# Seven block products in place of eight in the first feed-forward matrix, with two of four weight sums made by adding transfers

## The chip, the core and the metric

The kernel runs on one core of a Trainium2 chip. Its engines work side by side and are tied by semaphores: TensorE (PE) multiplies and writes to PSUM, VectorE (DVE) and ScalarE (ACT) work on elements, GpSimd (POOL) does the same more slowly and issues some transfers, SyncE (SP) only issues transfers. The metric is device microseconds (us) of one call, the median of several runs.

## What is computed

```python
def swiglu(x, w_in, w_out):
    gate, up = jnp.split(x @ w_in, 2, axis=-1)          # 1024 -> 2 x 2816
    return (jax.nn.silu(gate) * up) @ w_out             # 2816 -> 1024

def encoder_layer(x, ...):                              # DEPTH = 2
    x = layer_norm(ALPHA * x + 0.5 * swiglu(x, w_ffn_in[0], w_ffn_out[0]), ...)
    ...                                                 # pooling, short convolution, differential attention
    x = layer_norm(ALPHA * x + mix @ w_out, ...)
    x = layer_norm(ALPHA * x + 0.5 * swiglu(x, w_ffn_in[1], w_ffn_out[1]), ...)
```

There are 512 prompt tokens and 32 tokens of a second request, 544 in all, and all of it is float32. Two layers with two feed-forward blocks each make four feed-forward blocks; `w_ffn_in` of one block is 1024 x 5632.

## The kernel before

Activations stand with features on the partitions: 8 tiles `x[k]` of 128 x 544, worked on in two token halves `HS[0]` and `HS[1]` of 272 columns. For precision every operand is split into a high and a low part (`whi`, `wlo`, `xh`, `xl`), and a product is three matmuls: `whi*xh`, `wlo*xh`, `whi*xl` (`mm_h`, `mm_l`). Every matmul of these phases has 128 x 128 weights and 272 columns.

A feed-forward block walks over 22 slices of 128 hidden features (`i` in `ffn`). For each slice it multiplies the gate tile and the up tile of the first matrix: two tiles, two halves, 8 `k`, 3 matmuls, 96 in all. ACT takes silu of the gate (`sg`), DVE multiplies with the up part (L449), and the result is split into `hh` and `hl`. After 8, 7 and 7 slices (`FSPLIT`) the second matrix is multiplied for these slices and added to the residual `y` (one tile `ya` for all `k`). The last such phase is `out_phase`, which interleaves the layer norm `LN`, and `start` begins the next matrix while the normed `x` is still being made.

`Weights` streams the weights: SP loads a tile into one of two `raw` buffers, `group` makes a high part of 512 columns on ACT (L159) and a low part on DVE (L160), in rings of `W_BUFS` = 8 buffers. A ring buffer is written again when the matmuls of the group 8 places earlier have ended. The order of instructions on an engine is set at build time by a scheduler, and each engine executes its list in that order; an instruction that waits holds up everything behind it on its engine.

Of the kernel before, what the change touches and what calls it, by code (L numbers as in the profile page):

```python
# [16 lines left out]
P = 128  # L17
# [11 lines left out]
NF = D_FF // P  # L29
FSPLIT = (8, 7, 7)  # L30
NB = 2
W_BUFS = 8
# [16 lines left out]
UW = 640  # L49

# [17 lines left out]
def encoder_kernel(  # L68
# [28 lines left out]
    tp = ctx.enter_context(tc.tile_pool(name="tp", bufs=4))  # L97
# [46 lines left out]

    class Weights:


        def __init__(self, specs):
            self.specs, self.used, self.loaded, self.ready = specs, 0, 0, []

        def fetch(self):
            self.loaded += 1
            return wp.tile([P, NK * P], F32, tag="raw", name="raw", bufs=RAW_BUFS)

        def group(self, raw, g, n):
            e = min(G, n - g)
            hi = wp.tile([P, G], F32R, tag="whi", name="whi", bufs=W_BUFS)
            lo = wp.tile([P, G], F32R, tag="wlo", name="wlo", bufs=W_BUFS)
            S.activation(out=hi[:, :e], in_=raw[:, g:g + e], func=AF.Copy)  # L159
            V.tensor_tensor(out=lo[:, :e], in0=raw[:, g:g + e], in1=hi[:, :e].bitcast(F32), op=ALU.subtract)  # L160
            return hi, lo

        def load(self):
            src, n = self.specs[self.loaded]
            raw = self.fetch()
            nc.sync.dma_start(out=raw[:, :n], in_=src)
            self.ready.append([self.group(raw, g, n) for g in range(0, n, G)])

        def first(self, x):

            specs = self.specs[:2]
            raws = [self.fetch() for _ in specs]
            self.ready = [[], []]
            for i in range(NK // 4):
                ks, cs = slice(4 * i, 4 * i + 4), slice(i * G, (i + 1) * G)
                nc.sync.dma_start(out=ya[:, ks, HS[0]], in_=xT[:, ks, HS[0]])
                for (src, n), raw in zip(specs, raws):
                    nc.sync.dma_start(out=raw[:, cs], in_=src[:, cs])
                for k in range(NK)[ks]:
                    split(y[k], x[k], HS[0])  # L180
                for raw, out in zip(raws, self.ready):
                    out.append(self.group(raw, i * G, NK * P))
            nc.sync.dma_start(out=ya[:, :, HS[1]], in_=xT[:, :, HS[1]])

        def ahead(self, n):

            while self.loaded < min(self.used + n, len(self.specs)):
                self.load()

        def get(self, n=2):  # L190
# [3 lines left out]

    def mm_h(acc, w, x, k, h, first):

        cs = slice((k % 4) * P, (k % 4) * P + P)
        for i, v in enumerate(w[k // 4]):
            PE.matmul(acc[:, :HALF], v[:, cs], x[k][0][:, HS[h]], start=first and i == 0, stop=False)  # L199

    def mm_l(acc, w, x, k, h, last):

        cs = slice((k % 4) * P, (k % 4) * P + P)
        PE.matmul(acc[:, :HALF], w[k // 4][0][:, cs], x[k][1][:, HS[h]], start=False, stop=last)  # L204
# [30 lines left out]

    class LN:
# [9 lines left out]
        def ln_tile(self, name):  # L246
            return tp.tile([P, T], F32, tag="ln", name=name, bufs=3)

        def half_tile(self, tag, name, bufs):
            return tp.tile([P, HALF], F32, tag=tag, name=name, bufs=bufs)  # L250
# [29 lines left out]
        def add_last(self, m, acc, h):  # L280
            c, q = y[m][:, HS[h]], self.half_tile("z", "sq", 4)
# [23 lines left out]
        def spread(self, h, psum):  # L305

            d = self.half_tile("dg", "diag", 2)[:CH].rearrange("p (c t) -> p c t", c=NCH)
# [10 lines left out]
        def scale(self, h, k):  # L318
            l, j, sl = self.l, self.j, HS[h]
            c = y[k][:, sl]  # L320
            z = self.half_tile("z", "z", 4)
# [25 lines left out]
    def out_phase(l, j, x, ks, alpha):  # L347
# [4 lines left out]
        first = NK - nb  # L352
        for m in range(first):
# [37 lines left out]
        if ln.final:  # L391
# [7 lines left out]
            mean = ln.half_tile("dg", "mean", 2)  # L399
# [13 lines left out]
    def start(x, step, hooks, done):  # L413

        ws = [W.get(0), W.get(0)]
        accs = [(bank(), bank()), (bank(), bank())]
        todo = [(h, k) for h in range(2) for k in range(NK)][done:]
        for h in range(2):
            for k in range(NK):
# [8 lines left out]
                if h == 1 and k in (3, 6):  # L428
                    W.ahead(k // 3)
# [4 lines left out]

    def ffn(l, f, x, pre):
        for s, n in enumerate(FSPLIT):
            hs = []
            for i in range(n):
                if pre:
                    ga, ua = pre  # L440
                    pre = None
# [542 lines left out]
```

## Time and profile before

| what | value |
|---|---|
| median of 3 runs | 2107.07 us (2106.86 to 2107.29) |
| the profiled execution | 2106.86 us, of which the span from first to last instruction is 2104.7 us |
| PE busy | 2079.3 us, 99% of the span |
| DVE busy | 1013.1 us, 48% |
| ACT busy | 771.6 us, 37% |
| POOL busy | 228.8 us, 11% |
| moved by transfers | 189.13 MB, 90 GB/s on average |

Busy time of an engine adds up its instructions, which overlap a little on each engine because they are pipelined. The prediction is made against the span; 2.2 us of the profiled execution lie outside it.

### The profile page before, as it was taken

The numbers are of one execution on the slowest core, as the hardware profiler recorded it, in microseconds if no ns is written. First come the engines' busy times: TensorE is split into PE (matmuls) and PEld (weight loads), VectorE is DVE, ScalarE is ACT, GpSimd is POOL, SyncE is SP. The second block draws the span as 40 slices with busy tenths as digits, with TensorE's granted clock in tenths as the row PEclk, the third lists the DMA queues.
The fourth block names the chain that finished last, engine by engine and source line by source line (L and its number), as shares of the span: only waits on it lengthen the run. The fifth ranks groups of instructions, "written<-read, shape, count | busy, mean of one in ns | idle before, by whom it ended". The sixth has DMA issues, their size and how long they took to land.

```text
span 2104.7 us, 38545 instructions
## 1 busy us (share of the span) xinstructions
PE 2079.3 (99%) x16286; PEld 2042.2 (97%) x16286; DVE 1013.1 (48%) x1970; ACT 771.6 (37%) x1591; POOL 228.8 (11%) x216
## 2 busy tenths in 40 slices
PE   9999999999999999999999999999999999999997
PEld 9999999999999999999999999999999999999997
DVE  4333333776556333333653333347766553333337
ACT  5323223565435323223443232235653353222233
POOL 0000000511133000000420000006011320000003
PEclk9999999999999999999999999999999999999999
DMA  7322222132232222222232222222321222222221
GB/s 240 99 91 83 90 91 84 59 115 92 62 119 81 91 86 86 84 98 82 70 101 83 89 88 89 89 85 67 109 93 54 78 91 82 90 89 82 91 83 61
DMA packets 61749, 189.13 MB, mean 90 GB/s; under 512 B 8932, under 2 KB 13156, under 8 KB 61576
## 3 DMA queue, kind: packets, MB, share of 16 engines
q1 hardware_dynamic: 52592, 173.18, 25.9%
q10 hardware_dynamic: 8984, 13.49, 2.0%
q8 instruction: 128, 2.10, 0.4%
q14 instruction: 45, 0.37, 0.1%
HBM read 179.88 MB, written 8.34 MB: 89 GB/s over the span
## 4 chain that ended last, share of the span: by engine, by line
PE 95%; DVE 2%; POOL 1%; ACT 1%; issue 1%; DMA 0%; SPq 0%; POOLq 0%; ACTq 0%
PE b L199 59%; PE b L204 30%; PE b L629 1%; PE b L628 1%; PE o L644 1%; POOL xl L333 1%; PE b L609 0%; ACT ya L327 0%; DVE z L322 0%; PE b L716 0%; POOL rstd L302 0%; PE b L682 0%; DVE diag L308 0%; DVE acc L286 0%; PE b L311 0%
## 5 line engine op out<-in xcount | busy, mean ns | idle before, releaser
L199 PE MATMUL b<-xh,whi 128*128 128x272 f32 x3456 | 1000.0, 291 | 6.2 <-ACT xh L332 3.7
L199 PE MATMUL b<-xh,wlo 128*128 128x272 f32 x3456 | 993.5, 289 | 0.3 <-DVE wlo L160 0.3
L204 PE MATMUL b<-xl,whi 128*128 128x272 f32 x3456 | 978.2, 288 | 0.2
L160 DVE TENSOR_TENSOR wlo<-raw,whi 128x512 fp32r<-128x512 f32 (+1 forms) x656 | 469.7, 719 | 694.8 <-ACT whi L159 692.7
L159 ACT ACTIVATE whi<-raw 128x512 fp32r<-128x512 f32 (+1 forms) x656 | 403.3, 619 | 858.7 <-PE b L204 569.8
L199 PEld LDWEIGHTS b<-xh,whi 128*128 128x128 f32 x3456 | 651.7, 189 | 9.5 <-ACT xh L332 5.9
L199 PEld LDWEIGHTS b<-xh,wlo 128*128 128x128 f32 x3456 | 653.1, 189 | 1.5 <-DVE wlo L160 0.8
L204 PEld LDWEIGHTS b<-xl,whi 128*128 128x128 f32 x3456 | 644.6, 188 | 2.1 <-POOL xl L333 1.5
L199 PE MATMUL b<-hh,wlo 128*128 128x272 f32 x1408 | 406.2, 289 | 0.0
L199 PE MATMUL b<-hh,whi 128*128 128x272 f32 x1408 | 405.2, 288 | 0.0
L204 PE MATMUL b<-hl,whi 128*128 128x272 f32 x1408 | 404.6, 287 | 0.0
L199 PEld LDWEIGHTS b<-hh,wlo 128*128 128x128 f32 x1408 | 264.9, 188 | 0.2
L204 PEld LDWEIGHTS b<-hl,whi 128*128 128x128 f32 x1408 | 264.9, 188 | 0.2
L199 PEld LDWEIGHTS b<-hh,whi 128*128 128x128 f32 x1408 | 264.9, 188 | 0.0
L278 POOL TENSOR_TENSOR ya<-ya,shift 128x544 f32<-128x544 f32 x14 | 24.8, 1792 | 1412.9 <-DVE wlo L160 1386.4
L448 ACT ACTIVATE sg<-b 128x272 f32<-128x272 f32 x176 | 69.6, 397 | 213.1 <-PE b L204 213.0
L449 DVE SCALAR_TENSOR_TENSOR sg<-b,sg 128x272 f32<-128x272 f32 x176 | 77.6, 441 | 130.9 <-PE b L204 119.2
L343 DVE SCALAR_TENSOR_TENSOR ya<-ya,b 128x272 f32<-128x272 f32 x88 | 38.5, 438 | 88.7 <-PE b L204 87.8
L333 POOL TENSOR_TENSOR xl<-ya,xh 128x272 fp32r<-128x272 f32 x80 | 70.3, 901 | 30.8 <-ACT xh L332 25.1
L345 DVE TENSOR_TENSOR ya<-ya,b 128x272 f32<-128x272 f32 x108 | 46.7, 433 | 54.0 <-PE b L204 53.8
L232 ACT ACTIVATE hh<-sg 128x544 fp32r<-128x544 f32 (+1 forms) x100 | 59.1, 591 | 32.6 <-DVE sg L449 32.5
L233 DVE TENSOR_TENSOR hl<-sg,hh 128x544 fp32r<-128x544 f32 (+1 forms) x100 | 65.2, 652 | 7.2 <-ACT hh L232 7.1
(183 smaller groups left out, 1455.9 us busy)
## 6 DMA issues: line engine op xcount, KB each, us to landing
raw<-in_w SPq DMA_DIRECT2D x206, 512.0 KB, 3.5
raw<-in_w SPq DMA_DIRECT2D x64, 448.0 KB, 3.3
raw<-in_wi SPq DMA_DIRECT2D x40, 512.0 KB, 3.5
raw<-in_wo SPq DMA_DIRECT2D x16, 512.0 KB, 3.5
U<-scr ACTq DMA_DIRECT2D x8, 320.0 KB, 4.8
out_nkT<-k ACTq DMA_DIRECT2D x8, 272.0 KB, 2.1
out_nvT<-vT ACTq DMA_DIRECT2D x8, 272.0 KB, 2.1
out_yT<-ya SPq DMA_DIRECT2D x16, 136.0 KB, 1.8
```

What stands on the lines that cost most here:

```text
L159: S.activation(out=hi[:, :e], in_=raw[:, g:g + e], func=AF.Copy)
L160: V.tensor_tensor(out=lo[:, :e], in0=raw[:, g:g + e], in1=hi[:, :e].bitcast(F32), op=ALU.subtract)
L199: PE.matmul(acc[:, :HALF], v[:, cs], x[k][0][:, HS[h]], start=first and i == 0, stop=False)
L204: PE.matmul(acc[:, :HALF], w[k // 4][0][:, cs], x[k][1][:, HS[h]], start=False, stop=last)
L232: S.activation(out=hh[:, sl], in_=t[:, sl], func=AF.Copy)
L233: (eng or V).tensor_tensor(out=hl[:, sl], in0=t[:, sl], in1=hh[:, sl].bitcast(F32), op=ALU.subtract)
L278: POOL.tensor_tensor(out=c, in0=c, in1=self.s, op=ALU.subtract)
L333: POOL.tensor_tensor(out=xl[:, sl], in0=c, in1=xh[:, sl].bitcast(F32), op=ALU.subtract)
L343: V.scalar_tensor_tensor(out=c, in0=c, scalar=ALPHA, in1=a, op0=ALU.mult, op1=ALU.add)
L345: V.tensor_tensor(out=c, in0=c, in1=a, op=ALU.add)
L448: S.activation(out=sg[:, sl], in_=g[:, :HALF], func=AF.Silu)
L449: V.scalar_tensor_tensor(out=sg[:, sl], in0=u[:, :HALF], scalar=0.5, in1=sg[:, sl], op0=ALU.mult, op1=ALU.mult)
```

## The change

The matrix of one slice is cut into blocks: two token halves of `x`, two halves of the contraction (`k` 0 to 3, `e`; `k` 4 to 7, `o`), and up and gate. Slices 0 and 1 of a block (`NPLAIN` = 2) keep the eight block products. The other 20 slices use seven, each of 4 `k` and 3 matmuls, 12 matmuls. For that, sums are formed of the activations, once per feed-forward block (`Blocks`: `s56`, `s73`), and of the weight blocks, once per slice (`Weights.sums`): two by a transfer that POOL issues and that adds to what is already in its target (`accum_op`), two by DVE (`add`). A slice now has seven weight groups instead of four, and the ring has 9 buffers. The seven products go into three PSUM banks, one of which is read and then accumulated further (`seven`, `hidden`). One slice of the next split is computed ahead of each phase of the second matrix (`plan`). Tiles of the sums share memory with the tiles of attention and are allocated and released around it (`big["pool"]`).

```diff
-W_BUFS = 8
+NPLAIN = 2
+W_BUFS = 9
+XB = 18
...
+        def add(self, a, b):
+            r = big["pool"].tile([P, G], F32, tag="sum", name="sum", bufs=2)
+            V.tensor_tensor(out=r, in0=a, in1=b, op=ALU.add)
+            return r
+
+        def sums(self, src):
+            r13 = big["pool"].tile([P, 2 * G], F32, tag="r13", name="r13", bufs=2)
+            nc.sync.dma_start(out=r13, in_=src[:, :2 * G])
+            r11 = big["pool"].tile([P, G], F32, tag="b11", name="b11", bufs=2)
+            nc.sync.dma_start(out=r11, in_=src[:, :G])
             raw = self.fetch()
+            nc.sync.dma_start(out=raw, in_=src[:, 2 * G:])
+            POOL.dma_start(out=r13, in_=src[:, G:3 * G], accum_op=ALU.add)
+            b22, b21, r1, r3 = raw[:, :G], raw[:, G:], r13[:, :G], r13[:, G:]
+            g11, g21 = self.group(r11), self.group(b21)
+            r2 = self.add(r1, b22)
+            g2, g1 = self.group(r2), self.group(r1)
+            g3 = self.group(r3)
+            g22 = self.group(b22)
+            return g11, g21, g2, g1, g3, g22, self.group(self.add(r2, b21))
...
+    class Blocks:
+        def add(self, e, o):
+            h0, h1 = HS
+            t1, t2 = tmp("s56"), tmp("s73")
+            V.tensor_tensor(out=t1[:, h0], in0=e[:, h1], in1=o[:, h1], op=ALU.subtract)
+            V.tensor_tensor(out=t1[:, h1], in0=t1[:, h0], in1=e[:, h0], op=ALU.subtract)
+            V.tensor_tensor(out=t2[:, h0], in0=e[:, h0], in1=e[:, h1], op=ALU.subtract)
+            V.tensor_tensor(out=t2[:, h1], in0=o[:, h0], in1=t1[:, h1], op=ALU.add)
+            s = [new_b(n) for n in ("s56", "s73")]
+            split(t1, s[0])
+            split(t2, s[1])
+            self.sums.append(s)
+        def products(self):
+            e, o = self.plain[:NK // 2], self.plain[NK // 2:]
+            s56, s73 = ([s[i] for s in self.sums] for i in range(2))
+            for xs, h in ((e, 0), (o, 0), (s56, 1), (s56, 0), (s73, 0), (s73, 1), (o, 1)):
+                yield [tuple(v[:, HS[h]] for v in x) for x in xs]
+
+    def seven(ws, blocks, after):
+        banks = {}
+        for i, (w, xs, name) in enumerate(zip(ws, blocks.products(), "abacaca")):
+            opens = name not in banks
+            acc = banks.setdefault(name, bank() if opens else None)
+            for j, (xh, xl) in enumerate(xs):
+                cs = slice(j * P, (j + 1) * P)
+                for m, (v, x) in enumerate(((w[0], xh), (w[1], xh), (w[0], xl))):
+                    PE.matmul(acc[:, :HALF], v[:, cs], x, start=opens and j == 0 and m == 0,
+                              stop=j == len(xs) - 1 and m == 2, skip_group_check=True)
+            after[i](acc[:, :HALF])
...
+    def hidden(ws, blocks):
+        copy = lambda out: lambda acc: S.activation(out=out, in_=acc, func=AF.Copy)
+        def times(u, sl):
+            V.scalar_tensor_tensor(out=sg[:, sl], in0=u, scalar=0.5, in1=sg[:, sl], op0=ALU.mult, op1=ALU.mult)
+        def c12(acc):
+            V.tensor_tensor(out=sg[:, h0], in0=acc, in1=sg[:, h0], op=ALU.subtract)
+            S.activation(out=sg, in_=sg, func=AF.Silu)
+            times(up, h0)
+        seven(ws, blocks, [
+            copy(up),
+            lambda acc: V.tensor_tensor(out=up, in0=acc, in1=up, op=ALU.add),
+            copy(sg[:, h0]),
+            copy(sg[:, h1]),
+            lambda acc: V.tensor_tensor(out=sg[:, h1], in0=sg[:, h1], in1=acc, op=ALU.subtract),
+            c12,
+            lambda acc: times(acc, h1),
+        ])
+        return sg
...
     def ffn(l, f, x, pre):
+        xb = Blocks(x)
+        hs = []
+        for what, i in plan():
...
+                    sg = hidden(W.get(), xb)
...
-        with tc.tile_pool(name=f"at{l}", bufs=1) as ap:
-            x, pre = mixer(l, x, pre, ap)
+        big["pool"].release()
+        with tc.tile_pool(name=f"at{l}", bufs=1, reuse_waits="tile") as ap:
+            mix = mixer(l, x, pre, ap)
+        big["pool"] = tc.alloc_tile_pool(name="xb", bufs=1, reuse_waits="tile")
+        x, pre = out_phase(l, 1, mix, (4, 5, 6, 0, 1, 2, 3, 7), True)
```

The order of ACT's instructions in the stretch of seven-product slices decides when a PSUM bank is read. Before, one slice (hidden features of `sg_850`) stands on ACT as follows; `whi` are high parts of coming weights.

```order
L448 ACTIVATE sg_850<-b_740 128x272
L159 ACTIVATE whi_861<-raw_859 128x512
L448 ACTIVATE sg_850<-b_741 128x272
L159 ACTIVATE whi_865<-raw_859 128x512
L159 ACTIVATE whi_921<-raw_919 128x512
L159 ACTIVATE whi_925<-raw_919 128x512
L232 ACTIVATE hh_851<-sg_850 128x544
```

Now one slice (`sg_731`) stands there like this; `b_733` is the bank that four of its products share, `b_774` the one of two, and L558 are the copies out of them after the first, third and fourth product.

```order
L174 ACTIVATE whi_709<-sum_707 128x512
L558 ACTIVATE up_732<-b_733 128x272
L174 ACTIVATE whi_713<-r13_692 128x512
L174 ACTIVATE whi_717<-r13_692 128x512
L558 ACTIVATE sg_731<-b_733 128x272
L174 ACTIVATE whi_721<-raw_696 128x512
L558 ACTIVATE sg_731<-b_774 128x272
L174 ACTIVATE whi_727<-sum_725 128x512
L174 ACTIVATE whi_840<-b11_835 128x512
L565 ACTIVATE sg_731<-sg_731 128x544
L174 ACTIVATE whi_844<-raw_837 128x512
L292 ACTIVATE hh_829<-sg_731 128x544
```

A high part now stands ahead of the first copy, and silu and the split of the result share the queue with the parts of the next two slices. DVE had this order for one slice before (the low parts `wlo`, the two multiplications L449, the split L233):

```order
L160 TENSOR_TENSOR wlo_991<-raw_988,whi_990 128x512
L160 TENSOR_TENSOR wlo_995<-raw_988,whi_994 128x512
L449 SCALAR_TENSOR_TENSOR sg_979<-b_929,sg_979 128x272
L160 TENSOR_TENSOR wlo_1051<-raw_1048,whi_1050 128x512
L449 SCALAR_TENSOR_TENSOR sg_979<-b_930,sg_979 128x272
L160 TENSOR_TENSOR wlo_1055<-raw_1048,whi_1054 128x512
L233 TENSOR_TENSOR hl_981<-sg_979,hh_980 128x544
```

and has this one now, from the first weight sum of one slice to that of the next:

```order
L206 TENSOR_TENSOR sum_848<-r13_833,raw_837 128x512
L570 TENSOR_TENSOR up_732<-b_747,up_732 128x272
L175 TENSOR_TENSOR wlo_714<-r13_692,whi_713 128x512
L175 TENSOR_TENSOR wlo_718<-r13_692,whi_717 128x512
L175 TENSOR_TENSOR wlo_722<-raw_696,whi_721 128x512
L573 TENSOR_TENSOR sg_731<-sg_731,b_733 128x272
L175 TENSOR_TENSOR wlo_728<-sum_725,whi_727 128x512
L206 TENSOR_TENSOR sum_866<-sum_848,raw_837 128x512
L564 TENSOR_TENSOR sg_731<-b_774,sg_731 128x272
L175 TENSOR_TENSOR wlo_841<-b11_835,whi_840 128x512
L561 SCALAR_TENSOR_TENSOR sg_731<-up_732,sg_731 128x272
L561 SCALAR_TENSOR_TENSOR sg_731<-b_733,sg_731 128x272
```

and behind these:

```order
L175 TENSOR_TENSOR wlo_845<-raw_837,whi_844 128x512
L293 TENSOR_TENSOR hl_830<-sg_731,hh_829 128x544
L175 TENSOR_TENSOR wlo_851<-sum_848,whi_850 128x512
L206 TENSOR_TENSOR sum_989<-r13_974,raw_978 128x512
```

Fifteen instructions stand where seven stood. The last reader of the buffer `r13_692` is `wlo_718`; the next contents of that buffer are `r13_974`, and `sum_989`, their first reader, stands 12 places behind.

On SP three loads per slice stand where two stood, and POOL adds one transfer per slice that waits for the load of the same buffer (semaphores in brackets):

```order
L213 DMA b11_976<-in_w1 128x512 [waits DMAHW7_49,DMAHW5_49,DVE_49]
L211 DMA r13_974<-in_w1 128x1024 [waits DMASW2_49,DVE_49]
L215 DMA raw_978<-in_w1 128x1024 [waits DMAHW1_49,DVE_49]
...
L216 DMA r13_974<-in_w1 128x1024 [waits DMAHW6_49,DMASW2_49,DVE_49]
```

The first three are SP's, the last is POOL's; before, POOL issued no transfers.

## Rows read from the trace of the kernel before

**Rows 1.** The page's head, its busy times of all engines, the granted clock of PE in 40 slices (tenths of full speed), the main transfer queue (packets, MB, share of 16 engines) and the chain that ended last by engine.

```profile
span 2104.7 us, 38545 instructions
PE 2079.3 (99%) x16286; PEld 2042.2 (97%) x16286; DVE 1013.1 (48%) x1970; ACT 771.6 (37%) x1591; POOL 228.8 (11%) x216
PEclk9999999999999999999999999999999999999999
q1 hardware_dynamic: 52592, 173.18, 25.9%
PE 95%; DVE 2%; POOL 1%; ACT 1%; issue 1%; DMA 0%; SPq 0%; POOLq 0%; ACTq 0%
```

**Rows 2.** What PE waited for: us in total, times, longest wait.

```profile
PE b L311 <- DVE diag L308: 8.2, 6, 2.9
PE b L199 <- ACT xh L332: 3.7, 7, 1.0
```

**Rows 3.** Timeline (start, us, engine, line) of PE in a slice of the first matrix: three matmuls in a row, the first of them the last of a token half, and beside them ACT's silu that waits for that half.

```profile
60.22 0.29 PE L204 MATMUL b<-xl,whi 128*128 128x272 f32 x1
60.35 0.29 PE L199 MATMUL b<-xh,whi 128*128 128x272 f32 x1
60.47 0.29 PE L199 MATMUL b<-xh,wlo 128*128 128x272 f32 x1
60.55 0.40 ACT L448 ACTIVATE sg<-b 128x272 f32<-128x272 f32 x1 [1.77 <-PE b L204]
```

**Rows 4.** Timeline of ACT over one slice; idle time ahead of a row and what ended it stand in brackets.

```profile
62.09 0.63 ACT L159 ACTIVATE whi<-raw 128x512 fp32r<-128x512 f32 x1 [1.14 <-PE b L204]
63.53 0.40 ACT L448 ACTIVATE sg<-b 128x272 f32<-128x272 f32 x1 [0.81 <-PE b L204]
69.59 0.63 ACT L159 ACTIVATE whi<-raw 128x512 fp32r<-128x512 f32 x1 [0.87 <-PE b L204]
70.13 0.64 ACT L232 ACTIVATE hh<-sg 128x544 fp32r<-128x544 f32 x1
72.55 0.40 ACT L448 ACTIVATE sg<-b 128x272 f32<-128x272 f32 x1 [1.77 <-PE b L204]
84.55 0.40 ACT L448 ACTIVATE sg<-b 128x272 f32<-128x272 f32 x1 [1.77 <-PE b L204]
```

**Rows 5.** Timeline of DVE: a low part behind its high part, a low part with the split right behind it, then pairs of equal instructions back to back, first with POOL idle, then with POOL at work.

```profile
62.75 0.70 DVE L160 TENSOR_TENSOR wlo<-raw,whi 128x512 fp32r<-128x512 f32 x1 [3.17 <-ACT whi L159]
70.26 0.69 DVE L160 TENSOR_TENSOR wlo<-raw,whi 128x512 fp32r<-128x512 f32 x1 [0.28 <-ACT whi L159]
70.87 0.72 DVE L233 TENSOR_TENSOR hl<-sg,hh 128x544 fp32r<-128x544 f32 x1
...
662.88 1.29 DVE L160 TENSOR_TENSOR wlo<-raw,whi 128x512 fp32r<-128x512 f32 x2
...
651.81 0.78 DVE L316 TENSOR_TENSOR ya<-ya,b 128x272 f32<-128x272 f32 x2
656.82 1.86 DVE L160 TENSOR_TENSOR wlo<-raw,whi 128x512 fp32r<-128x512 f32 x2
```

**Rows 6.** Groups of instructions by line and shape: count, busy us, mean ns of one.

```profile
L160 DVE TENSOR_TENSOR wlo<-raw,whi 128x512 fp32r<-128x512 f32 x592 | 427.5, 726 | 677.1 <-ACT whi L159 675.0
L449 DVE SCALAR_TENSOR_TENSOR sg<-b,sg 128x272 f32<-128x272 f32 x176 | 77.6, 441 | 130.9 <-PE b L204 119.2 <-ACT sg L448 3.9
```

**Rows 7.** Transfers by line: count, KB each, median us from issue to landing.

```profile
raw<-in_w SPq DMA_DIRECT2D x206, 512.0 KB, 3.5
U<-scr ACTq DMA_DIRECT2D x8, 320.0 KB, 4.8
ya<-in_xT SPq DMA_DIRECT2D x1, 1088.0 KB, 8.6
```

**Rows 8.** Four slices of the first matrix as one stretch: us, busy us of PE, PEld, DVE, ACT and POOL (instructions), granted clock, share of the 16 DMA engines, GB/s.

```profile
168.00:216.00 48.00, 48.00 (x387) 48.00 (x386) 17.19 (x28) 15.03 (x28) 0.00 (x0) 1.00 0.28 87
```

**Rows 9.** Timeline at the end of a layer norm, ahead of the second feed-forward block of layer 0: POOL, ACT (the last normed tiles L327, silu of slice 0 and of slice 1) and DVE (the last centred tiles).

```profile
656.12 0.77 DVE L322 TENSOR_TENSOR z<-ya,b 128x272 f32<-128x272 f32 x2
657.61 0.40 ACT L448 ACTIVATE sg<-b 128x272 f32<-128x272 f32 x1
658.23 1.11 ACT L327 ACTIVATE ya<-z,par_sb 128x272 f32<-128x272 f32 x2
661.86 0.40 ACT L448 ACTIVATE sg<-b 128x272 f32<-128x272 f32 x1 [0.84 <-PE b L204]
674.99 0.40 ACT L448 ACTIVATE sg<-b 128x272 f32<-128x272 f32 x1 [1.83 <-PE b L204]
652.25 5.89 POOL L333 TENSOR_TENSOR xl<-ya,xh 128x272 fp32r<-128x272 f32 x6 [0.28 <-ACT xh L332]
```

**Rows 10.** Timeline around the beginning of attention in layer 0: ACT's queue with the issues of the bias transfers, far ahead of their use, and DVE's first reader of such a tile.

```profile
39.36 0.78 ACTq L524 DMA_DIRECT2D Us<-scr  x2
43.28 1.07 ACTq L536 DMA_DIRECT2D U<-scr  x2
424.99 1.15 ACT L159 ACTIVATE whi<-raw 128x512 fp32r<-128x512 f32 x2 [0.62 <-DMA raw<-in_wi]
433.72 1.29 DVE L630 SCALAR_TENSOR_TENSOR sc<-b,U 128x512 f32<-128x512 f32 x2
```

More of the change, by code (lines that the diff above doesn't have):

```diff
@@ new lines, in load @@
+        def load(self):
+            kind, src, n = self.units[self.loaded]
+            self.loaded += 1
+            if kind == "t":
+                raw = self.fetch()
+                nc.sync.dma_start(out=raw[:, :n], in_=src)
+                out = Tile([self.group(raw[:, g:min(g + G, n)]) for g in range(0, n, G)])
+            elif kind == "p":
+                out = self.pair([self.group(b) for b in self.blocks(src)])
+            else:
+                out = self.sums(src)
+            self.ready.append(out)
@@ L193, in get, with two @@
             return self.ready.pop(0)
+        def two(self):
+            return self.get(0) if self.units[self.used][0] == "p" else [self.get(0), self.get(0)]
     def mm_h(acc, w, x, k, h, first):
-        cs = slice((k % 4) * P, (k % 4) * P + P)
-        for i, v in enumerate(w[k // 4]):
-            PE.matmul(acc[:, :HALF], v[:, cs], x[k][0][:, HS[h]], start=first and i == 0, stop=False)
+        for i, v in enumerate(w.at(k)):
+            PE.matmul(acc[:, :HALF], v, x[k][0][:, HS[h]], start=first and i == 0, stop=False)
     def mm_l(acc, w, x, k, h, last):
-        cs = slice((k % 4) * P, (k % 4) * P + P)
-        PE.matmul(acc[:, :HALF], w[k // 4][0][:, cs], x[k][1][:, HS[h]], start=False, stop=last)
+        PE.matmul(acc[:, :HALF], w.at(k)[0], x[k][1][:, HS[h]], start=False, stop=last)
     def mm(acc, w, x, ks, h):
@@ L413, in start @@
     def start(x, step, hooks, done):
-        ws = [W.get(0), W.get(0)]
+        ws = W.two()
         accs = [(bank(), bank()), (bank(), bank())]
@@ new lines, in plan @@
+    def plan():
+        ends = [sum(FSPLIT[:s + 1]) for s in range(len(FSPLIT))]
+        for i in range(NF):
+            yield 1, i
+            if i in ends:
+                yield 2, ends.index(i)
+        yield 2, len(FSPLIT) - 1
+    def ffn(l, f, x, pre):
+        xb = Blocks(x)
+        hs = []
+        for what, i in plan():
+            if what == 1:
+                if i < NPLAIN:
+                    ua, ga = pre if i == 0 else [run(mm2(w, x, range(NK))) for w in W.get()]
+                    sg = tmp("sg")
+                    for sl, g, u in zip(HS, ga, ua):
+                        S.activation(out=sg[:, sl], in_=g[:, :HALF], func=AF.Silu)
+                        V.scalar_tensor_tensor(out=sg[:, sl], in0=u[:, :HALF], scalar=0.5, in1=sg[:, sl],
+                                               op0=ALU.mult, op1=ALU.mult)
+                else:
+                    sg = hidden(W.get(), xb)
+                hs.append(new_x("h"))
+                split(sg, hs[-1])
+                continue
+            n = FSPLIT[i]
+            part, hs = hs[:n], hs[n:]
+            if i == len(FSPLIT) - 1:
+                return out_phase(l, 2 * f, part, range(n), False)
+            for m in range(NK):
+                acc = run(mm2(W.get(), part, range(n)))
+                for h in range(2):
+                    resid(m, acc[h], h, i == 0)
```

143 lines of the change are left out of this document (74 added, 69 removed).

## Prediction

> **What bounds the kernel now.** I read the page's busy times first, then the chain that ended last, then what PE waited for, then the timeline of one slice. PE is busy for 99% of the span at full granted clock, and the chain runs over PE for 95% of it [rows 1]. PE's own waits are small: the largest is 8.2 us over 6 waits, the next 3.7 us [rows 2]. So time goes only where matmuls go, or where a new wait comes in. In the timeline a matmul starts 0.125 us after the one before (60.22, 60.35, 60.47) though it lasts 0.29 [rows 3], and silu of the same half comes back every 12.00 us (60.55, 72.55, 84.55) [rows 3, 4]: 96 matmuls of 0.125 us and no gap. DVE has 17.2 us and ACT 15.0 us of work in 48 us of such slices [rows 8], so both have room. That room is what the change spends.
>
> **What is removed.** A seven-product slice has 7 x 12 = 84 matmuls in place of 96, of the same shape. At 0.125 us this is 10.5 us in place of 12.0, 1.5 us less. There are 20 such slices in each of 4 blocks, 80 in all: **-120.0 us**. The order of the built program agrees, PE has 960 matmuls fewer. I expect 0.125 us to hold, since each matmul still brings its own weights, as before.
>
> **What ACT and DVE get.** Per slice DVE has 7 low parts and 2 sums of 512 columns, 5 operations of 272 and a split of 544. Back to back, a low part frees DVE after 0.61 us (70.26 to 70.87), an operation of 272 after 0.35 (0.78 for two, each 0.43 long) [rows 5]; the split I put at 0.64. That is 9 x 0.61 + 5 x 0.35 + 0.64 = 7.9 us of 10.5, 75%. ACT has 7 high parts at 0.54 (69.59 to 70.13), three copies at about 0.3, silu and a split at about 0.6 [rows 4]: 5.9 us. Neither is the bound by its sum, so the order counts.
>
> Call the products P0 to P6, 1.5 us each, and the end of P0 zero. P2 adds into the bank of P0, so it needs the copy out of it. On ACT a high part, waiting for the same end of P0, stands ahead of the copy: 0.04 us from PE to ACT (60.51 to 60.55 [rows 3]), 0.54, then 0.40, then 0.04 back, 1.02 us. P2 would start 1.33 us after P0's end (12 matmuls and a start later, less the last one's 0.29), so there are 0.31 us to spare. P4 behind P2's copy stands the same. The longer chain ends in the same place one slice later: P4 ends at 6.0; high part to 6.67, low part and second sum on DVE to 7.92, subtraction to 8.36, silu to 9.04, two multiplications to 9.86, split on ACT, which is free again at 10.44; the high part behind it may start at 10.54. That leaves 0.10 us there, 0.41 in all. Behind the wait stand, on ACT, the copies that PE needs. I take 0.05 us per slice lost, **+4 us**, between 0 and 0.4 us (32 us).
>
> **The adding transfer.** This is the unknown. The buffer `r13` of a slice is last read by the low part of its fourth half: P2 ends at 3.0, high part to 3.67, low part to 4.39. Then SP loads it anew, 3.5 us from issue to landing [rows 7], with signals to 7.95. Only then POOL may issue the adding transfer, which takes A. Its first reader is a sum on DVE, at 11.81 by DVE's order (0.67 for the high part behind P0 of the next slice, 0.03, 0.61 for its low part). A up to 3.9 us costs nothing. Behind a late sum stand on DVE an addition, three low parts and the subtraction that frees P4's bank for P6. They take 3.3 us and P6 starts at 7.3 of its slice, so the sum may start at 4.0 after P0's end instead of 1.3 before PE notices. But a late sum also frees the next `r13` late: from its start 2.26 us to the end of that low part, then 3.56, then A. This loop takes A + 5.8 us and must fit in 10.5, so beyond A = 4.7 each slice slips by A - 4.7. Slices run in stretches of 7, 7 and 6 per block, and the first two of each have their sums made during other work. With five loads in a stretch of 7 the first sum starts at A - 2.55, four slips follow, and PE loses 5A - 25.3 us; in a stretch of 6 it loses 4A - 20.7. There are 8 and 4 such stretches.
>
> The trace has no adding transfer. The nearest row is a plain load of the same 512 KB, 3.5 us; that is the lower end. Its share can be split: 28% of the 16 engines over 12 us of a slice with two such loads [rows 8] makes 1.7 us of moving for one, so 1.8 us are fixed. If the target is read as well as the source, moving doubles: 5.2 us. The far end is 8.6 us, which a transfer of 1088 KB took beside others [rows 7]. I take 5.2, since adding must fetch the target's old contents. Then a stretch of 7 loses 0.7 us and one of 6 0.15: **+6 us**. At 3.5 it is 0, at 6.0 51 us, at 7.0 107 us, at 8.6 197 us.
>
> The Trainium skill ("DMA: Bandwidth & Descriptors", section "Anatomy of one DMA — SWDGE (gpsimd) path") gives transfers issued by GpSimd 2.0 us plus bytes over 436 GB/s, an estimate of 3.2 us here; by it the sum would have no loop term and end near 1999. No run here shows it for a transfer that adds.
>
> **Start of a feed-forward block.** The sums of `x` are 16 operations at 0.35 and 8 splits at 0.64, 10.7 us of DVE, four times. They begin when the last normed halves come, near 656.9 [rows 9]. In DVE's order 16 sums, six splits and two low parts (10.6 us) stand ahead of slice 0's multiplications, and six splits ahead of its silu on ACT. Before, that silu ran at 657.61. Slice 0 holds 4 of 6 PSUM banks until then, and slice 1, from 661.9 on, needs its third bank 6 us later, at 667.9; DVE comes there at 667.5. The first product with a sum of `x` is due at 676.9 and these are ready by about 671. So they are covered by slice 1, almost exactly; I put **+4 us**, 1 us each, between 0 and 3. Without that cover each would cost up to its 10.7 us.
>
> **Attention's tiles** now share memory with the sums, so the bias transfers, issued at 39 to 44 us before, are issued when the layer norm has ended: five issues of 0.39 to 0.54 us on ACT's queue, then 4.8 us to land [rows 7, 10]. From 425 this is 432, before their reader at 433.7 [rows 10]. The issues hold ACT up by 2.1 us, twice: **+4 us**, between 0 and 10.
>
> Second matrix, projections and layer norm keep their instructions; the ninth buffer and the slice computed ahead I cost at nothing, because PE does not wait there now [rows 2].
>
> **Sum.** 2104.7 - 120.0 + 4 + 6 + 4 + 4 = 2002.7 us of span; with 2.2 us outside, **2005 us**. The profiled execution's 2106.86 is 0.2 below the median of 2107.07, which is nothing here.
>
> **Rivals.**
> *The loop sets the pace in part* (A between 5.5 and 7): at 6.2 the stretches lose 5.7 and 4.1 us, 62 us in place of 6, 2061 us. For it: every load shares the engines with 1.84 MB per slice where there was 1.05. Against it: 28% of the engines were taken [rows 8], with the new bytes at most about 70%.
> *DVE is slowed.* With POOL at work (six operations from 652.25 to 658.14 [rows 9]) two low parts take 1.86 us instead of 1.29 [rows 5]; the mean over all is 0.726 against 0.70 alone [rows 5, 6]. POOL now prepares a transfer in each slice. If that eats the 0.41 us to spare and 0.4 us more, 80 x 0.4 = 32 us in place of 4: 2033 us. Against it: preparing a transfer isn't an operation on tiles.
> *Slower than before.* The adding transfer takes over 7.0 us, and the loop gives the 120 us back; at 8.6 it is 2104.7 - 120 + 12 + 197 + 2.2 = 2196 us. For it: DVE is busy 75% of a slice, and DVE and POOL visibly get in each other's way [rows 5], so the transfer's preparation could wait for DVE. The Trainium skill ("SBUF — State Buffer", section "SBUF: two separate sides") has such a rule: GpSimd cannot write a transfer's descriptors while DVE holds the port pair they share, in its two-port modes, and a transfer of 0.62 us took 3.1. Whether the operations here do that no row shows. Against it: low parts and sums have two inputs each, and only their slowdown, not POOL's, is in the rows.
>
> **Chances.** Forecast (A up to 5.5, 1984 to 2030): 0.60. Loop in part: 0.15. DVE slowed: 0.12. Slower: 0.11. No change by chance between these: 0.02. A measurement here tells 0.2%, 4 us, from nothing. Faster 0.87, same 0.02, slower 0.11. With no wait at all the sum is 1987; some of PE's old waits (11.9 us in the two rows [rows 2]) may go too, so the low end is 1984. The high end is 2066, A of 6.3, which leaves out the slower case and the upper half of the second: about 0.8 inside.
>
> **What would show it.** Right: the first copy of a slice every 10.5 us, PE at 98% or more, the adding transfer landing 5 us after issue, and DVE's first weight sum waiting under 1 us. Wrong: the sums waiting for POOL's transfer for several microseconds and growing along a stretch (loop), low parts above 0.8 us (DVE slowed), PE waiting for ACT's copy in every slice (my order of ACT is too kind), or PE waiting for `xh`-type splits at a block's start.

## The result and the profile after

The changed kernel took **2131.18 us** (median of four runs, 2124.77 to 2132.99) where the kernel before took 2106.97 (2105.69 to 2107.29): a ratio of 1.0111, 95% interval 1.0089 to 1.0132. It is slower by 24 us; forecast was 2005, and the range, 1984 to 2066, doesn't hold it.

The page of the changed kernel, to be read against [rows 1]: its head and busy times, the granted clock in 40 slices, and the issues of transfers (count, size, median us to landing).

```profile
span 2128.6 us, 38056 instructions
PE 2003.1 (94%) x15326; PEld 1944.5 (91%) x15326; DVE 1371.8 (64%) x2694; ACT 997.6 (47%) x2009; POOL 297.1 (14%) x296
PEclk8999999999999999999999999999999999999998
...
r<-in_w SPq DMA_DIRECT2D x80, 512.0 KB, 3.8
r<-in_w POOLq DMA_DIRECT2D x80, 512.0 KB, 6.1
```

The 960 matmuls are gone, PE's busy time fell by 76 us, and yet the span grew: PE now stands idle for 125 us, 25 before (the page counts the time of overlapping instructions once, so the rest of the span is idle time). The adding transfer (the POOLq row) lands after 6.1 us. What PE waited for stands in the second view (us in total, times, longest), to be compared with [rows 2], where the largest was 8.2 us:

```profile
PE b L348 <- DVE sg L573: 68.3, 43, 3.0
PE b L260 <- ACT xh L449: 11.4, 9, 2.5
PE b L260 <- ACT sg L597: 10.7, 4, 7.5
PE b L428 <- DVE diag L425: 7.7, 6, 2.9
```

The first row is new: in 43 slices the last product waits for DVE's subtraction that frees its bank (`sg`, L573). The third is new too: slice 1 of a block waits for slice 0's silu, 7.5 us of it at one place. DVE's own waits say what the subtraction stands behind ("issue" is a wait whose end the view couldn't put down to an instruction):

```profile
DVE sum L206 <- issue: 150.4, 37, 5.3
DVE sum L206 <- DMA r<-in_w: 33.0, 10, 4.7
```

So the first sum of a slice's weights waits for the adding transfer, 47 times, 3.9 us each; by the landings in the trace it starts 0.08 us after that transfer has landed. One turn of it, in the second stretch of block 1 (timelines of SP's queue, POOL, DVE and PE; idle time ahead of a row and what ended it in brackets):

```profile
198.81 0.33 SPq L211 DMA_DIRECT2D r<-in_w  x1
203.10 0.86 POOL L216 DMA_DIRECT2D r<-in_w  x1 [13.66 <-DVE sg L561]
208.95 0.69 DVE L206 TENSOR_TENSOR sum<-r,raw 128x512 f32<-128x512 f32 x1 [3.92 <-issue]
209.91 1.28 DVE L175 TENSOR_TENSOR wlo<-r,whi 128x512 fp32r<-128x512 f32 x2
211.22 0.33 SPq L211 DMA_DIRECT2D r<-in_w  x1
211.72 0.43 DVE L573 TENSOR_TENSOR sg<-sg,b 128x272 f32<-128x272 f32 x1
212.20 0.40 PE L348 MATMUL b<-xh,whi 128*128 128x272 f32 x1 [1.41 <-DVE sg L573]
...
221.65 0.69 DVE L206 TENSOR_TENSOR sum<-r,raw 128x512 f32<-128x512 f32 x1 [4.19 <-issue]
```

SP reloads `r13` at 198.81; POOL issues the adding transfer 4.29 us later, 0.56 us after the reload has landed (the view puts POOL's wait down to DVE, but what the issue awaits of DVE, the reload had awaited too); 5.85 us after that the sum starts on DVE, having waited 3.92. Behind it stand the two low parts that free the `r13` of the slice before, and 2.27 us after the sum's start SP reloads that buffer. That is the loop of the prediction: 4.29 + 5.85 + 2.27 = 12.41 us from reload to reload, in a slice whose matmuls need 10.5. The subtraction is late with it, and PE waits 1.41 us.

The whole stretch, seven slices, in the view by stretches (us; busy us of PE, PEld, DVE, ACT, POOL; granted clock, DMA share, GB/s): 81.69 us for what should be 7 x 10.5 = 73.5, at full granted clock, with DVE busy 67% and ACT 54% of the time.

```profile
178.24:259.93 81.69, 75.72 (x590) 73.98 (x589) 54.47 (x101) 43.84 (x83) 5.19 (x6) 1.00 0.57 150
```

The stretch lengths, read from PE's timeline as first matmul (in blocks 1 to 3 the first behind the layer norm's mean) to first matmul of what follows, give the account. Two plain slices with seven others need 97.5 us, seven others 73.5, six others 63. The first stretches of the four blocks took 123.0, 113.1, 114.9 and 119.0; the second 81.7, 84.0, 84.9 and 81.3; the third 69.1, 69.1, 68.9 and 69.7. Over their need, and less what the kernel before lost in the same places (6.7 us at its starts), that is 73 + 38 + 24 = 135 us. The ends of the layer norms add 3, attention 4. With -120 this makes 22 of the 24 us.

### The profile page after: what moved, and what is told of

The parts are those of the page before. It is cut to its first block, busy times and chain, and to the rows that moved or that the text cites. A ratio compares the mean times of both kernels' runs of the same rounds, so it can differ in the third digit from the quotient of the medians.

```text
span 2128.6 us, 38056 instructions
## 1 busy us (share of the span) xinstructions
PE 2003.1 (94%) x15326; PEld 1944.5 (91%) x15326; DVE 1371.8 (64%) x2694; ACT 997.6 (47%) x2009; POOL 297.1 (14%) x296
## 4 chain that ended last, share of the span: by engine, by line
PE 68%; DVE 13%; issue 8%; DMA 7%; ACT 3%; POOL 2%; ACTq 0%; DVEq 0%; SPq 0%; POOLq 0%
PE b L260 26%; PE b L348 23%; PE b L264 13%; DVE wlo L175 5%; DMA r<-in_w 4%; DMA raw<-in_w 2%; PE b L779 1%; PE b L778 1%; POOL xl L450 1%; ACT whi L174 1%; DVE sg L561 1%; PE o L794 1%; DVE up L570 1%; DVE sg L573 1%; ACT ya L444 1%
## 5 line engine op out<-in xcount | busy, mean ns | idle before, releaser
L174 ACT ACTIVATE whi<-raw 128x512 fp32r<-128x512 f32 x496 | 302.4, 614 | 452.0 <-PE b L264 331.8
L175 DVE TENSOR_TENSOR wlo<-raw,whi 128x512 fp32r<-128x512 f32 x496 | 340.4, 689 | 218.2 <-ACT whi L174 215.5
L348 PE MATMUL b<-xh,whi 128*128 128x272 f32 x960 | 286.2, 298 | 68.4 <-DVE sg L573 68.3
L260 PE MATMUL b<-xh,whi 128*128 128x272 f32 x896 | 268.1, 304 | 24.7 <-ACT xh L449 11.4
L348 PE MATMUL b<-xh,wlo 128*128 128x272 f32 x960 | 281.1, 293 | 0.0
L348 PE MATMUL b<-xl,whi 128*128 128x272 f32 x960 | 280.2, 292 | 0.0
L260 PE MATMUL b<-xh,wlo 128*128 128x272 f32 x896 | 258.9, 293 | 0.3 <-DVE wlo L175 0.3
L348 PEld LDWEIGHTS b<-xh,whi 128*128 128x128 f32 x960 | 185.8, 193 | 78.2 <-DVE sg L573 78.0
L264 PE MATMUL b<-xl,whi 128*128 128x272 f32 x896 | 245.7, 293 | 2.2 <-POOL xl L450 2.2
L216 POOL DMA_DIRECT2D r<-in_w x80 | 69.7, 871 | 1268.3 <-DVE sg L561 474.7
L260 PEld LDWEIGHTS b<-xh,whi 128*128 128x128 f32 x896 | 173.0, 193 | 31.1 <-ACT xh L449 15.6
L348 PE MATMUL b<-s56h,whi 128*128 128x272 f32 x640 | 188.5, 295 | 4.6 <-ACT up L558 4.6
L348 PE MATMUL b<-s73h,whi 128*128 128x272 f32 x640 | 185.1, 289 | 6.6 <-ACT sg L558 6.6
L348 PEld LDWEIGHTS b<-xh,wlo 128*128 128x128 f32 x960 | 185.9, 194 | 0.0
L348 PEld LDWEIGHTS b<-xl,whi 128*128 128x128 f32 x960 | 185.5, 193 | 0.0
```

The costliest lines, as they stand in the source:

```text
L174: S.activation(out=hi[:, :n], in_=raw, func=AF.Copy)
L175: V.tensor_tensor(out=lo[:, :n], in0=raw, in1=hi[:, :n].bitcast(F32), op=ALU.subtract)
L216: POOL.dma_start(out=r13, in_=src[:, G:3 * G], accum_op=ALU.add)
L260: PE.matmul(acc[:, :HALF], v, x[k][0][:, HS[h]], start=first and i == 0, stop=False)
L264: PE.matmul(acc[:, :HALF], w.at(k)[0], x[k][1][:, HS[h]], start=False, stop=last)
L348: PE.matmul(acc[:, :HALF], v[:, cs], x, start=opens and j == 0 and m == 0, stop=j == len(xs) - 1 and m == 2, skip_group_check=True)
```

## Experiments

Each kernel is the changed one with the edit shown. Beside each group ran the kernel before (2106.9 to 2109.5 us median).

**Opening the loop by order.** The order of DVE puts the first sum of a slice ahead of the low parts that free the other `r13`; it can stand there because there are two `sum` buffers. With one buffer, and the second sum written over the first, it can't stand so early.

```
-        def add(self, a, b):
-            r = big["pool"].tile([P, G], F32, tag="sum", name="sum", bufs=2)
+        def add(self, a, b, r=None):
+            if r is None:
+                r = big["pool"].tile([P, G], F32, tag="sum", name="sum", bufs=1)
...
-            return g11, g21, g2, g1, g3, g22, self.group(self.add(r2, b21))
+            return g11, g21, g2, g1, g3, g22, self.group(self.add(r2, b21, r2))
```

> The two sums that DVE makes share one buffer, the second written over the first, so that the first sum of a slice can no longer stand on DVE ahead of the two low parts that free the r13 of the slice before. No transfer and no operation is taken away. Theory of the loop (late sum on DVE, low parts that free r13 2.3 us behind it, reload 4.3 us, adding transfer 6.1 us, next late sum: 12.7 us where a slice needs 10.5): the loop is opened, a slice comes back every 10.4 us, the time falls by about 95 us from 2131 to 2036 (2025 to 2050). Rival, DVE and ACT are too full for 10.5 us: slices stay above 12 us, time within 15 us of 2131. Rival, the transfers crowd each other: half of the gain, 2060 to 2100.

Measured: **2030.57 us** (2026.23 to 2031.65), ratio to before 0.963 (0.9614 to 0.9645), 100.6 us below the changed kernel. The timelines of DVE, SP and ACT now show both low parts of `r`, then the reload, and 3.0 us after it the next slice's sum, with no wait ahead of it; the silu of a slice (L566) comes 10.51 us after the one before:

```profile
193.90 0.68 DVE L175 TENSOR_TENSOR wlo<-r,whi 128x512 fp32r<-128x512 f32 x1
195.00 0.69 DVE L175 TENSOR_TENSOR wlo<-r,whi 128x512 fp32r<-128x512 f32 x1 [0.42 <-ACT whi L174]
195.72 0.33 SPq L212 DMA_DIRECT2D r<-in_w  x1
198.74 0.69 DVE L207 TENSOR_TENSOR sum<-r,raw 128x512 f32<-128x512 f32 x1
199.81 0.66 ACT L566 ACTIVATE sg<-sg 128x544 f32<-128x544 f32 x1 [0.34 <-DVE sg L565]
210.32 0.66 ACT L566 ACTIVATE sg<-sg 128x544 f32<-128x544 f32 x1 [0.35 <-DVE sg L565]
```

The stretch of seven slices that took 81.69 us, in the same view:

```profile
168.60:242.35 73.75, 73.75 (x590) 73.59 (x589) 56.52 (x101) 43.70 (x83) 5.18 (x6) 1.00 0.66 166
```

And the adding transfer on the page, with PE's wait for the subtraction (L574 here) in the view of waits:

```profile
r<-in_w POOLq DMA_DIRECT2D x80, 512.0 KB, 7.3
...
PE b L349 <- DVE sg L574: 0.4, 1, 0.4
```

The stretch takes 73.75 us, and PE's wait for the subtraction went from 68.3 us to 0.4. The adding transfer even got longer, and PE loses nothing by it. No transfer and no operation was removed, so neither DVE or ACT being too full nor the crowding of transfers set the pace: the loop did.

**Without the adding transfer.**

```
-            POOL.dma_start(out=r13, in_=src[:, G:3 * G], accum_op=ALU.add)
```

> The adding transfer is left out, so r13 holds only the first blocks and two of the seven products are of other numbers; everything else stays, the place of the first sum on DVE too. Theory of the loop: it shrinks from 12.7 to 2.3 + 4.3 = 6.6 us, under the 10.5 of a slice: 2036 us (2025 to 2050), like the run with the sum written in place. Rival, DVE and ACT too full: no change, 2115 to 2135. Rival, crowding of the transfers: clearly faster than the run with the sum in place, which keeps all transfers, by 15 us or more.

Measured: 2017.59 us (2014.66 to 2020.27), under the expected 2025 to 2050 and 13 us below the run before. So the loop is gone here too. Of the further 13 us some 7 lie at the blocks' starts (first stretches 1 to 2 us shorter each), the others in the rest of the program. The 512 KB more per slice, by crowding or on POOL, may be what costs them, but DVE's order differs between the two runs as well; it was not taken apart.

**Overwriting instead of adding.**

```
-            POOL.dma_start(out=r13, in_=src[:, G:3 * G], accum_op=ALU.add)
+            POOL.dma_start(out=r13, in_=src[:, G:3 * G])
```

> The second transfer stays on POOL's queue with the same 512 KB, but overwrites instead of adding, so two products are of other numbers. If adding is what makes it long (the target has to be read), it lands in about 4.2 us in place of 6.1, as the plain loads beside it do, the loop is 10.8 us and the time near 2045. If the way over POOL is what costs, it lands in 6 us again and the time stays at 2125 to 2135. Loop theory in both cases: the period of a slice is the landing time plus 6.6 us, or 10.5 if that is more.

Measured: 2046.97 us (2044.23 to 2049.88). The same bytes over the same queue land in 4.6 us, 1.5 less than when they are added (issues on the page, then DVE's wait for the sum):

```profile
r<-in_w SPq DMA_DIRECT2D x80, 512.0 KB, 3.8
r<-in_w POOLq DMA_DIRECT2D x80, 512.0 KB, 4.6
...
DVE sum L206 <- issue: 75.5, 30, 3.5
```

That makes the loop 11.2 us, still over 10.5, and the second stretches take 75.4 to 76.0 us, 2.3 over their need. So 1.5 us of landing time were worth 84 us of the program, 56 times as much, which is the number of loads in the prediction's formula (five in 8 stretches, four in 4).

**Rings of 8, and a third buffer for r13.** The memory for a third buffer is taken from the rings of 9; both runs have rings of 8 and are read against each other.

```
-W_BUFS = 9
+W_BUFS = 8
```

> The changed kernel with rings of 8 in place of 9 for the halves of the weights, and nothing else. Loop theory: the loop of 12.7 us is not made of these rings, so 2131 again (2122 to 2145). Rival, the rings set the pace: with one buffer less each high part waits for a product 1.5 us later and the time rises by 80 slices x 1 us or so, 2180 and more.

Measured: 2181.23 us (2175.6 to 2183.15). The expectation of 2131 missed, and the rival's 2180 came: one buffer less costs 50 us. What of it is the ring's own is read below. With it also

```
-            r13 = big["pool"].tile([P, 2 * G], F32, tag="r13", name="r13", bufs=2)
+            r13 = big["pool"].tile([P, 2 * G], F32, tag="r13", name="r13", bufs=3)
```

> Three buffers for r13, with the memory taken from the rings of weight halves (8 in place of 9); it is read against the run that has the rings of 8 alone. Loop theory: with a third buffer the late sum of a slice has two slices (21 us) for its 12.7, so the 95 us go as with the sum in place: about 2040 us, 85 to 100 below the run with rings of 8 alone. Rival, it was not the buffer but something else that the sum in place moved (the order of the low parts on DVE): within 20 us of the run with rings of 8 alone.

Measured: **2045.55 us** (2043.45 to 2053.98), 136 us below, more than the 85 to 100 expected. That fits a loop that costs more with rings of 8: the second stretches take 85.6 to 87.7 us there, 81.3 to 84.9 with rings of 9. What PE waited for in the two, first the rings of 8 alone:

```profile
PE b L348 <- DVE sg L573: 103.8, 55, 4.0
```

and then with the third `r13`:

```profile
PE b L348 <- DVE sg L573: 14.2, 9, 2.5
```

A second, unlike way of opening the same loop has the same effect. To see what the ring is worth without the loop, the sum in place was run with rings of 8 (both edits as above):

> The sum in place, with rings of 8. It tells whether the ring of 9 is worth anything once the loop is open. With the loop, one buffer less cost 50 us (2181 against 2131). If that came from the loop made longer by it, then within 10 us of the run with the sum in place (2031). If the rings are a limit of their own, 2060 or more; three buffers of r13 with rings of 8 gave 2046, so 2035 to 2050 is the likeliest.

Measured: 2047.87 us (2043.95 to 2048.28), the same as three buffers of `r13` to 2 us, and 17 above the ring of 9. So of the 50 us some 17 are the ring's own. For the rest there is a reading by the loop, not a test: the adding transfer landed in 6.6 us there, 0.5 more, and the reload reached POOL's issue 0.2 us later, which 56 times is 39 us. The mean granted clock also fell, from 0.982 to 0.967; what that cost was not taken apart.

**All four sums on DVE.**

```
-            nc.sync.dma_start(out=r13, in_=src[:, :2 * G])
+            nc.sync.dma_start(out=r13[:, G:], in_=src[:, G:2 * G])
...
-            POOL.dma_start(out=r13, in_=src[:, G:3 * G], accum_op=ALU.add)
...
+            V.tensor_tensor(out=r1, in0=r11, in1=r3, op=ALU.add)
+            V.tensor_tensor(out=r3, in0=r3, in1=b22, op=ALU.add)
```

> All four sums of weight blocks on DVE, no adding transfer, and 512 KB less to load for each slice. The loop is then 2.3 + 4.3 + two sums of 0.6, under 10.5. DVE has 1.2 us more per slice, 9.1 of 10.5. If DVE keeps up: 2020 us, as with the adding transfer left out (2017.6). If DVE is too full at 87%, PE waits in each slice for low parts, sums or the operations that free its banks, 0.5 to 1 us x 80: 2060 to 2100.

Measured: 2040.36 us (2038.83 to 2042.4), between the two expectations. The stretch takes 76.47 us, DVE busy 79% of it:

```profile
168.10:244.57 76.47, 74.88 (x591) 73.77 (x590) 60.73 (x111) 43.32 (x83) 0.00 (x0) 1.00 0.32 100
```

Two more sums per slice cost 2 to 3 us per stretch of seven, much less than the loop took. PE's wait that comes with them is the one for ACT's copy after a slice's first product (`up`), and ACT's timeline shows the split of the result, which stands two places ahead of that copy, waiting for DVE's multiplication:

```profile
PE b L349 <- ACT up L559: 9.4, 27, 0.8
...
180.57 0.66 ACT L293 ACTIVATE hh<-sg 128x544 fp32r<-128x544 f32 x1 [0.79 <-DVE sg L562]
181.14 0.62 ACT L174 ACTIVATE whi<-sum 128x512 fp32r<-128x512 f32 x1
181.66 0.38 ACT L559 ACTIVATE up<-b 128x272 f32<-128x272 f32 x1
```

That fits the prediction's longer chain, from the fifth product over DVE to the split on ACT, which had 0.10 us to spare: with two sums on DVE and the loop open PE waited for this copy 4 times, with four 27 times. Plain sums on DVE are 91 us better than the adding transfers as the change places them, and 10 worse than adding transfers with the loop open.

**The starts of the blocks.** Two runs price them without any seven-product slice:

```
-NPLAIN = 2
+NPLAIN = 22
```

> The changed kernel with all 22 slices of a block plain: no seven products, no sums of weight blocks, but the new plan, the shared memory of the layer norm and the attention, the ring of 9 and the sums of x (which nothing reads) stay. It prices what the change costs beside the products. Theory: the 25 to 30 us that remain at the block starts with the loop opened are there here too, since the sums of x stand ahead of slice 0's silu: 2107 + 25 to 30 + 5 for the layer norms = 2132 to 2142 us. Rival, they come with the first seven-product slices (their weights, their first sums): 2107 to 2115.

Measured: 2138.8 us (2138.33 to 2141.53), ratio 1.0145 (1.013 to 1.016): 29 us over before, as expected by the theory of the starts. The first stretches, nine slices of 12 us here, exceed their need by 18.8, 2.6, 1.9 and 2.4 us more than those of before, so it is not four equal starts: the program's own start has most of it. PE's largest waits in this run, and a row of ACT at its start:

```profile
PE b L260 <- ACT sg L597: 15.5, 4, 13.5
PE b L260 <- ACT xh L449: 11.4, 9, 2.5
...
37.98 0.63 ACT L174 ACTIVATE whi<-raw 128x512 fp32r<-128x512 f32 x1 [8.92 <-DMA raw<-in_w]
```

So the 13.5 us are not the sums of `x` alone: until 37.98 ACT stood idle for 8.92 us for a load of weights, whose high part stands ahead of five of the splits and of the silu. The run overprices the program's start of the changed kernel, which has no such wait for weights there, and that the total is the expected one is in part chance.

The same with the sums of `x` behind slice 0's activation:

```
-        xb = Blocks(x)
...
+                if i == 0:
+                    xb = Blocks(x)
```

> The same with the sums of x written behind slice 0's activation. If the silu of slice 0 standing behind those sums is what delays a block's start, 10 to 20 us less than the run with all slices plain, down to 2112 to 2120 with 5 left for the layer norms. If the sums cost nothing in that order, the two runs agree within 4 us.

Measured: 2126.0 us (2124.56 to 2126.41), 12.8 less; the wait for slice 0's silu falls to 2.7 us, and 17 us stay (9.6 at the starts, the rest elsewhere, layer norms and attention among it). How the program's start looks in the changed kernel itself: ACT's and PE's timelines, and the two stretches of 12 us that hold them.

```profile
27.49 0.63 ACTq L631 DMA_DIRECT2D scr<-rows  x1
28.25 0.66 ACT L292 ACTIVATE s56h<-s 128x544 fp32r<-128x544 f32 x1 [3.31 <-DMA r<-in_w]
34.24 0.66 ACT L292 ACTIVATE s56h<-s 128x544 fp32r<-128x544 f32 x1 [1.32 <-DVE s L324]
34.92 1.28 ACT L597 ACT_TABLE_LOAD   x1
36.21 0.40 ACT L597 ACTIVATE sg<-b 128x272 f32<-128x272 f32 x1
36.66 0.59 PE L260 MATMUL b<-xh,whi 128*128 128x272 f32 x1 [7.47 <-ACT sg L597]
...
24.00:36.00 12.00, 5.20 (x42) 4.98 (x40) 10.39 (x25) 6.70 (x13) 1.92 (x2) 0.82 0.92 252
36.00:48.00 12.00, 11.34 (x72) 11.34 (x73) 11.45 (x21) 8.14 (x17) 0.86 (x1) 0.75 0.69 203
```

In the kernel before, the same silu and the first of the two stretches:

```profile
23.08 0.69 ACT L448 ACTIVATE sg<-b 128x272 f32<-128x272 f32 x2
...
24.00:36.00 12.00, 12.00 (x98) 12.00 (x98) 4.85 (x13) 6.30 (x12) 0.31 (x1) 1.00 0.73 195
```

The silu is 13.1 us later. Seven splits of the sums stand ahead of it on ACT, and the last of them, at 34.24, waits for DVE, whose sums of `x` run until 35.5. The splits also begin late: the issue of `scr<-rows`, which needs the transfer `rows<-vec` issued at 24.16, stands ahead of the first, and ACT is idle for 3.31 us until 28.25. (The view names another transfer there; in the run with the sum in place, where the same wait is 5.37 us, it names `rows<-vec`.) PE waits 7.47 us for its bank, and works at a granted clock of 0.75 in the 12 us behind. The edit in the changed kernel, with its loop:

> The sums of x are written behind the activation of slice 0 of a block instead of ahead of it, so that its silu and multiplications no longer stand behind some 11 us of sums on ACT and DVE; the loop stays. Theory: of the 136 us that the first matrices lost, some 35 lie at the four block starts, where slice 1 waits for slice 0's PSUM banks; these go, 2131 to about 2100 (2090 to 2110), and the wait of PE for slice 0's silu (10.7 us over 4) goes to under 1 us. Rival, the first slices of a block are late because their sums of x are late whatever the order: PE waits for the sums of x at slice 2 instead, 2120 to 2131.

Measured: 2117.84 us (2114.7 to 2119.32), 13.3 less, where 31 were expected. PE's wait for that silu went, but 4.6 us of waiting for a low part took its place at the program's start, and in the same stretch 4.0 us for a copy on ACT. Neither expectation held fully.

**Both edits.**

> The sum written in place and the later sums of x together. Alone they took 101 and 13 us off. If they are independent: 2031 - 13 = 2018 us (2010 to 2022). In the run with the sum in place the first stretches of the four blocks still take 30 us more than before beyond their matmuls; if the late silu of slice 0 is the whole of that and the loop took part of the gain back in the run with the loop, 2000 us. If the sums of x then come too late for slice 2 (4.6 us of such a wait at the program's start in that run), 2020 or more.

Measured: **2024.29 us** (2016.28 to 2025.41), ratio 0.9594 (0.9567 to 0.9621). It is the fastest of the versions that leave nothing out, 83 us under the kernel before and 107 under the changed one, but the second edit gave only 6 us beside the first, not 13: the first stretches still exceed those of before by 25 us. The 4.6 us for a low part at the program's start are there again; besides them single waits of 1 to 2.5 us for the layer norm's splits and for copies on ACT show. What the starts still cost was not taken apart.

## Why the prediction was wrong, point by point

- **960 matmuls at 0.125 us, -120: right.** With the loop open a stretch of seven takes 73.75 us, 10.54 a slice, and PE has no idle time in it.
- **Order of ACT and DVE, +4 (0 to 32): right.** The same stretch is 0.25 us over its need, some 3 us for 80 slices. "DVE is slowed" didn't come: a low part of 512 columns takes 0.682 to 0.709 us in the mean, by the tile it reads, 0.726 before [rows 6]. The chain that it left 0.10 us for is real: with two sums more on DVE, PE waits for ACT's copy.
- **The adding transfer, +6: the step that failed.** The mechanism and the form of the loop were as the prediction put them, but two of its terms were too small. The transfer took 6.1 us where 5.2 was taken; by the prediction's own formula that is 56 us. And the way from reload to POOL's issue took 4.2 to 4.4 us in most turns where [rows 7] had given 3.5 with 0.06 for signals: about 0.75 us more, so that slices slip beyond A = 3.95 and not 4.7, and 56 times 0.75 is another 42 us. The last piece, 2.26 us from the sum to the freed buffer, measured 2.27. With both corrected the formula gives 98 us; the run with the loop opened says 101. The rival "in part" held the right landing time (5.5 to 7) but took over the short reload, and so had 62 us and a chance of 0.15. Of the 0.75 us only some 0.3 lie in the load itself, 3.8 us (the engines were 57% busy where [rows 8] had 28%). The larger part passes behind it: by the landings in the trace POOL begins its issue 0.55 us after the reload has landed (0.54 to 0.58 in 65 of the 71 turns with a landing on record), where DVE's waiting sum begins 0.08 us after the adding transfer. The 0.06 for signals rested on no row of that kind, since POOL issued no transfers before. A loop over its limit multiplies each such error by 56.
- **What the prediction didn't ask** is why two buffers of `r13` behaved as one. The answer was in DVE's order, which it had used: the next slice's sum stands ahead of the low parts that free the other buffer, a full slice before that sum is needed. The loop was avoidable, and the run with the sum in place avoids it without any operation more.
- **Starts of the blocks, +4 (0 to 12): wrong.** With the loop open the first stretches exceed those of before by 13, 6, 5 and 6 us, 30 in all. Without the products the inner starts cost 2 to 3 us each, the upper end of what was allowed; by difference the first seven-product slices add about 3 each; a wait of 0.9 us for a copy on ACT at 689.4 in the changed kernel is one that shows. The program's start was the large miss: the cover by slice 1 was worked out at 657 us and carried over to the first block. There DVE's sums begin at 20.0, wait 3.5 us in between for a one-time result of ACT, their splits wait 3.3 us more behind a one-time transfer issue, and the sums end at 35.5, while slice 1 needs its third bank at 28.9. The cover was 7 us too short; PE waited 7.5 us, and 9.5 with the loop open.
- **Attention's tiles, +4: right** as a size (3 to 4 us from PE's timelines, by where the cut to the layer norm is made). The ends of the layer norms, forecast at nothing, cost 3.
- **The rival that ends slower** had the right sign for the wrong reason. It wanted POOL's issuing to wait for DVE and a transfer of over 7.0 us; the transfer took 6.1, and the longer way to its issue did the rest. The issue took 0.86 us at the least and 1.06 at the most over 80 transfers, with DVE busy 64%. The rule of the Trainium skill ("SBUF — State Buffer", section "SBUF: two separate sides") doesn't show in that time; whether any operation of DVE here is in the modes that it names, no row shows. By the formula of the Trainium skill ("DMA: Bandwidth & Descriptors", section "Anatomy of one DMA — SWDGE (gpsimd) path"), an estimate, the transfer would have taken 3.2 us; the trace has 6.1 with adding and 4.6 without.
- **What would show it.** Where the sum came late, the silu came mostly every 12.0 to 13.3 us, not 10.5, PE was busy 94%, and the sums waited 3.9 us. They did not grow along a stretch, as was written, since in a loop each turn is late by the same amount; what grows is how far PE is behind.

Together: the loop, 101 us by the run that opens it, was 95 us more than forecast, the four starts 26, the layer norms 3. That is 124 of the 126 us between 2005 and 2131.

## What to carry to other kernels

When a transfer waits for a buffer that an in-order engine frees behind work that itself waits for that transfer, write the loop down, and ask of each step whether it must stand there: one place in an order decided 100 us here, with DVE and ACT a third idle or more. Ask too what each hand-over costs: a landing was followed by POOL's issue only 0.55 us later. A forecast near such a limit needs a range from the loop's slope times the error of each term, not from the term's best guess. And work that is hidden at one block's start isn't hidden at the program's.

## What the runs showed of the hardware

- Adding to the target makes a 512 KB transfer over POOL's queue 1.5 us longer than overwriting it (6.1 against 4.6 us to landing), and POOL's own time to issue it goes from 0.53 to 0.86 us. In the run with the loop open, with the 16 engines busy 66% of a stretch in place of 57%, it took 7.3 us.
- POOL began the issue of a transfer 0.55 us after the landing that it waited for (0.54 to 0.58 us in 65 of 71 turns of the changed kernel, the same in the runs that overwrite and with the loop open). DVE began a sum that waited for a landing 0.08 us after it.
- Some of PE's waits were followed by time at the lower clock (1.2 in place of 2.4 GHz): the mean granted clock of the run was 0.994 before, 0.982 in the changed kernel, 0.986 with the loop open and 0.967 with rings of 8. In the stretch from 84 to 96 us, in which PE waited 2.1 us for the subtraction, it was 0.88; in the one shown from 178 to 260, with four waits of 6.0 us in all and 1.9 at the longest, it stayed at 1.00. What of the 24 us this makes was not measured by itself.
